# Weight tiles split over their whole width, and the products with a tile's low part issued last, in a diffusion layer on one Trainium2 core

## The chip, the cores and the metric

The kernel runs on one core of one Trainium2 chip. The metric is the device time of one execution in microseconds (us); the median of three runs counts. Engines are named as in the profile: PE is TensorE's matmul stream and PEld its weight loads, DVE is VectorE, ACT is ScalarE, POOL is GpSimd, SP is SyncE, which here only issues DMAs.

## What is computed

One layer of a diffusion backbone over 256 latent tokens and 256 context tokens, width 2048, all in float32: a half-step SwiGLU feed-forward block (FFN1, 5632 hidden channels), a token mixer (attention heads beside mLSTM heads), a second half-step feed-forward block (FFN2, latent tokens only), each behind an RMS norm whose shift, scale and gate come from a condition vector through `w_mod`.

```python
def half_step_ffn(x, mod, i, g, w_up, w_down):
    h = adaln(x, g, mod, i)
    a, b = jnp.split(h @ w_up, 2, axis=-1)
    return x + 0.5 * mod[:, i + 2, None, :] * ((jax.nn.silu(a) * b) @ w_down)
...
    mod_l = (silu_c @ w_mod[l] + b_mod[l]).reshape(B, N_MOD, D_MODEL)
    xl = half_step_ffn(xl, mod_l, 0, ...); xc = half_step_ffn(xc, mod_c, 0, ...)
    ...                                    # projections w_in, mLSTM, attention, w_out
    xl = half_step_ffn(xl, mod_l, 6, ...)
    return rms_norm(xl, g_final)
```

## The kernel before

**Products in three parts.** A float32 product is made of three matmuls on float32r operands (`mm3`, L138): each operand x is kept as hi (x rounded to float32r) and lo (x minus hi), and hi·hi, hi·lo and lo·hi are added up in one PSUM bank. Tokens are split once and kept; weights are split as they arrive. A weight tile is 128 x 2048, 1 MB, loaded by one DMA into one of three `raw` buffers (or accumulated by POOL's DMAs into one of two `chain` buffers, which hold sums of weight blocks).

**The split (L110).** `split` works on each half of the tile, 1024 wide: ACT copies the half to `hi` (L118), DVE subtracts (L119) to get `lo`. `hi` and `lo` have four buffers of 1024 each, so two tiles' worth. A buffer is free again when the last matmul that reads it is done.

**Two ways round.** With `hhi`/`hlo` (tokens) moving, the weights stand still; in the feed-forward blocks the tokens stand still and the weights move, 512 columns at a time. Per step of the contraction, `mm3` issues (token hi, weight hi), (token hi, weight lo), (token lo, weight hi).

**FFN1's quads.** Most of FFN1's first half (`quad`, called ten times, n = 1 to 10) makes four products of blocks out of seven (Strassen-Winograd form). A quad goes through seven entries `m`, each with two weight tiles `q`, so 14 tiles. For each tile the products of token block s = 0 are issued, then those of s = 1: 2 x 4 x 3 = 24 matmuls of 512 columns. The entries, their token forms, and the PSUM banks that they add to, two banks each (s = 0, 1):

```python
            order = (
                (a11, held, X, True, chained(1, 0), p1),
                (a12, plain, Z, True, None, c11),
                (n1, held, Y, True, chained(1, 2), kept),
                (s4, loaded, Y, False, lambda q: accum(ra[q], part(n, 1, q)), p35),
                (s2, held, X, False, chained(0, 2), c12),
                (s3, lambda q: ra[q], X, False, None, c22),
                (a22, held, Y, True, again, c21),
            )
```

The fourth value says whether the banks begin afresh. Two neighbours share banks: s4 adds to the Y that n1 has just filled, and s3 to the X that s2 has just filled. In between, the last function of the entry reads the bank: `kept(s)` is an ACT copy of Y to `cy` (L765); `c12(s)` is a DVE addition of X to `c12` (L744) and a multiplication (L745). So the first s4 matmul on Y[0] has to wait for `kept(0)`, and the first s3 matmul on X[0] for the addition of `c12(0)`. `c21(s)` at the quad's end is a DVE addition, an ACT Silu (L783) and a DVE multiplication; its result is transposed on PE by `turned()` (L739), called after the products of s = 0 in the first tile (q = 0) of an entry, so in the next quad's first tile for s = 0.

**Side work.** Beside the quads, DVE reduces tiles of `w_mod` (128 x 1024, `sraw`, two buffers, loaded by SP at L227): two `SCALAR_TENSOR_TENSOR` operations per tile (L198), one tile per step of a quad in most steps.

**What sets the order.** The kernel's framework lists each engine's instructions before the launch, by its own scheduler; on the chip each engine's list is fixed, with semaphore waits. At the start (before 150 us) PE and DVE are held to the order of the source.

**Other stages.** FFN1's second half (`pair`, five times) runs the same seven entries over two column blocks c, so that two neighbours on one bank have a whole tile of the other column block between them. The token projections (`project`, `channels`) follow, then the mixer, `out_proj`, and FFN2, where quads of one token block alternate with ordinary tiles (`units`).

Of the kernel before, what the change touches and what calls it, by code (L numbers as in the profile page):

```python
# [19 lines left out]
P = 128  # L20
# [29 lines left out]
def tile_layer(ctx: ExitStack, tc: tile.TileContext, I: dict, out: bass.AP):  # L50
# [59 lines left out]
    def split(raw, n=2048):  # L110

        half = n // 2
        parts = []
        for h in range(2):
            hi = wp.tile([P, 1024], F32R, tag="hi", name="hi", bufs=4)[:, :half]
            lo = wp.tile([P, 1024], F32R, tag="lo", name="lo", bufs=4)[:, :half]
            src = raw[:, h * half : (h + 1) * half]
            nc.scalar.activation(hi, src, AF.Copy)  # L118
            vector[0].tensor_tensor(lo, src, hi.bitcast(F32), op=ALU.subtract)  # L119
            parts.append((hi, lo))  # L120

        def at(w):
            h, o = divmod(w.start, half)
            return tuple(x[:, o : o + w.stop - w.start] for x in parts[h])

        return at
# [11 lines left out]
    def mm3(out_ap, sh, sl, mh, ml, first, last, skip=False):  # L138

        tensor[0].matmul(out_ap, sh, mh, start=first, stop=False, skip_group_check=skip)  # L140
        tensor[0].matmul(out_ap, sh, ml, start=False, stop=False, skip_group_check=skip)  # L141
        tensor[0].matmul(out_ap, sl, mh, start=False, stop=last, skip_group_check=skip)  # L142
# [257 lines left out]
    def products(wup, pre, k0, k1, hhi, hlo, early=False):  # L400

        n = (k1 - k0) * P
        most = min(2 * NPRE, 2048 // n // 2 * 2)

        def load(u0):
            nu = min(most, 2 * NPRE - u0)
            raw = raw_tile(n * nu)  # L410
            tc.keep_in_program_order(
                nc.sync.dma_start(
                    raw.rearrange("p (u c) -> p u c", u=nu),
                    wup[u0 // 2 : (u0 + nu) // 2, :, :, k0 * P : k1 * P].rearrange("f a p c -> p (f a) c"),
                )
            )
            return raw, nu

        ahead = load(0)
        if early:  # L420
            wt = split(ahead[0], n * ahead[1])
        yield
        for u0 in range(0, 2 * NPRE, most):
            raw, nu = ahead
            if u0 or not early:
                wt = split(raw, n * nu)
            if u0 + most < 2 * NPRE:
                ahead = load(u0 + most)
            for u in range(nu):
                b = pre[(u0 + u) // 2][u % 2]  # L430
                for k in range(k0, k1):
                    w = slice(u * n + (k - k0) * P, u * n + (k - k0 + 1) * P)
                    mm3(b, *wt(w), hhi[:, k, :], hlo[:, k, :], k == 0, k == KT - 1)
                yield
# [207 lines left out]
    with pool(name="f1u", bufs=1) as f1u:  # L642
# [26 lines left out]
        for f in range(NPRE, FB):  # L669
            pab = []  # L670
            for ab in range(2):
                wt = load_split(I["w_up1"][f, ab])
                b = bank()
                for k in range(KT):
                    mm3(b, *wt(slice(k * P, (k + 1) * P)), hhi[:, k, :], hlo[:, k, :], k == 0, k == KT - 1)
                pab.append(b)
            tail(f, pab)
# [72 lines left out]
        def quad(n, after=lambda step: None):  # L750
# [198 lines left out]
    def pair(p):  # L949
# [73 lines left out]
        for m, (g, src, dst, fresh, then, use) in enumerate(order):  # L1023
            a = place0[m] if p == 0 and m < 2 else place[g]
            for c in range(2):
# [8 lines left out]
                if p == NP - 1:  # L1034
# [5 lines left out]
                    if m in (1, 4, 6):  # L1040
                        gates = used[c] = ahead.pop(0)
                    elif m == 5:
                        gates = used[c]
                for s in range(2):
                    if fresh:
                        dst[c, s] = tbank() if c and dst is not X else bank()
                    for j in range(FB):
                        k = slice((FB * s + j) * P, (FB * s + j + 1) * P)
                        mm3(dst[c, s], a[:, 0, k], a[:, 1, k], *wt(slice(j * CB, (j + 1) * CB)), fresh and j == 0, j == FB - 1, True)
# [5 lines left out]
    def block_products(b, wt, t):  # L1055
        for j in range(FB):
            w = slice((FB * t + j) * P, (FB * t + j + 1) * P)
            mm3(b, hid10[0][:, w], hid10[1][:, w], *wt(slice(j * CB, (j + 1) * CB)), j == 0, j == FB - 1)
# [12 lines left out]
    def last1():  # L1071
# [3 lines left out]
        for s in (CTX, LAT):  # L1075
            for i, (_, cb) in [(i, x) for i, x in enumerate(LAST) if x[0] == s]:
# [7 lines left out]
                for t in range(2 * s, 2 * s + 2):  # L1084
                    b = bank()
                    block_products(b, wt, t)
# [18 lines left out]
    def products_of(bs, wt, n, ks, toks):  # L1105

        for j, k in enumerate(ks):
# [24 lines left out]
    with ExitStack() as mx:  # L1132
# [165 lines left out]
        def channels(name, h, N, b):  # L1298

            wt = load_split(I[name][h])  # L1300
            for k in range(KT):
                w = slice(k * P, (k + 1) * P)
                mm3(b, *wt(w), hhi[:, k, 512 - N :], hlo[:, k, 512 - N :], k == 0, k == KT - 1)
                if k % 4 == 3:
                    next(beside["part"], None)
                    yield
# [336 lines left out]
        def out_proj(cb, gs, bs):  # L1643
            bs.extend(bank() for _ in range(2))
            for n, g in enumerate(gs):
                wt = load_split(I["w_out"][cb, g])
                for j in range(4):
                    k = 4 * g + j
                    w = slice(j * CB, (j + 1) * CB)
                    for t in range(2):  # L1650
                        tt = slice(t * P, (t + 1) * P)
                        mm3(bs[t], chi2[:, k, tt], clo2[:, k, tt], *wt(w), n == 0 and j == 0, n == len(gs) - 1 and j == 3)
                    yield
# [109 lines left out]
    with f2x:  # L1763
# [28 lines left out]
        for f in range(NPRE, FB):  # L1792
            pab = []
            for ab in range(2):
                wt = load_split(I["w_up2"][f, ab])
                b = bank()[:, :T]
                for k in range(KT):
                    mm3(b, *wt(slice(k * P, (k + 1) * P)), h2hi[:, k, :T], h2lo[:, k, :T], k == 0, k == KT - 1)
# [110 lines left out]
        def quad(n):  # L1909
# [65 lines left out]
            for m, (a, src, dst, fresh, then, use) in enumerate(order):  # L1975
                for q in range(2):
# [3 lines left out]
                    if then:  # L1980
                        then(q)
                    for j in range(4):
                        k = 4 * q + j
                        mm3(B[dst], a[0][:, k, :], a[1][:, k, :], *wt(slice(j * CB, (j + 1) * CB)), fresh and k == 0, k == 7, True)
# [4 lines left out]
        def up(n):  # L1989

            sab = []
            for ab in range(2):
                bs = [bank() for _ in range(2)]
                for u in range(4):
                    wt = load_split(part(n, ab, u))
                    for j in range(4):
                        k = 4 * u + j
                        w = slice(j * CB, (j + 1) * CB)
                        for t in range(2):
                            tt = slice(t * P, (t + 1) * P)  # L2000
                            mm3(bs[t], h2hi[:, k, tt], h2lo[:, k, tt], *wt(w), k == 0, k == KT - 1)
# [10 lines left out]
        def block(n, wt, t):  # L2012

            b = bank()
            tt = slice(t * P, (t + 1) * P)
            for j in range(FB):
                w = slice(j * CB, (j + 1) * CB)
                mm3(b, hids[n][0][:, j, tt], hids[n][1][:, j, tt], *wt(w), j == 0, j == FB - 1)
            return b
# [3 lines left out]
        def down(n):  # L2023

            assert (n, 1) in done or not n
            for cb in range(NCB):
                wt = load_split(I["w_dn2"][n, cb])
                for t in range(2):
                    c = slice(cb * CB, (cb + 1) * CB)
                    b = block(n, wt, t)  # L2030
# [51 lines left out]
        def last2():  # L2082
# [13 lines left out]
            for t in range(2):  # L2096
                ss = sm.tile([P, 4], F32, tag="ss4", name="ss4", bufs=4)
                for cb in range(NCB):
                    c = slice(cb * CB, (cb + 1) * CB)
                    b = block(LAST, parts[cb], t)  # L2100
# [109 lines left out]
```

## Time and profile before

| | |
|---|---|
| three runs | 2667.7 us median (2666.27 to 2670.44) |
| span of the profiled execution | 2666.8 us, 0.9 us below the median; no other time is recorded for it |
| granted TensorE clock, mean | 0.996 |
| PE busy | 2609.9 us (98%), 12718 matmuls, each with a weight load of its own (PEld x12718) |
| DVE / ACT / POOL busy | 2130.1 us (80%) / 1347.2 us (51%) / 221.6 us (8%) |
| DMA | 679.97 MB, mean 255 GB/s |

A matmul's record lasts longer than the step to the next one, since matmuls overlap; the step is what counts. In a timeline, a row is start, duration, engine, line, operation, out<-in, and in brackets the idle time before it with what ended that.

### The profile page before, as it was taken

How to read it: one execution, taken by the hardware profiler on the slowest of the kernel's cores; microseconds unless marked ns; L12 is line 12 of the kernel's file. 1: busy time of each engine (PE TensorE's matmuls, PEld its weight loads, DVE VectorE, ACT ScalarE, POOL GpSimd, SP SyncE). 2: the span in 40 equal slices, each digit the busy share in tenths (PEclk: the TensorE clock that was granted, in tenths of full speed). 3: DMA queues.
4: the chain of work that ended last, by engine and by line, in shares of the span. 5: the costliest groups of instructions: out<-in, count | busy, mean ns of one | idle time of the engine just before them, and what ended most of it. 6: DMA issues, size and time to landing. Idle time of an engine off the chain costs nothing. (4 is left out here: it accounts for less than half of the span.)

```text
span 2666.8 us, 33730 instructions
## 1 busy us (share of the span) xinstructions
PE 2609.9 (98%) x12718; PEld 2158.4 (81%) x12718; DVE 2130.1 (80%) x2901; ACT 1347.2 (51%) x1682; POOL 221.6 (8%) x271
## 2 busy tenths in 40 slices
PE   8999999999999999999999999999999999999998
PEld 4688887888888878888889888877888888888886
DVE  5797878878888788888886979797688777777867
ACT  4354444544444565444454346355476655555554
POOL 0000001100000100000110000121000000000001
PEclk9999999999999999999999999999999999999999
DMA  9979999999999989889986866574579998989975
GB/s 346 351 213 270 263 279 260 258 276 281 264 280 273 266 230 239 229 209 234 225 233 224 309 229 225 205 260 166 172 249 284 295 286 292 289 277 281 277 230 168
DMA packets 135027, 679.97 MB, mean 255 GB/s; under 512 B 14152, under 2 KB 23624, under 8 KB 73552
## 3 DMA queue, kind: packets, MB, share of 16 engines
q1 hardware_dynamic: 107504, 500.59, 50.9%
q0 software_dynamic: 27360, 177.22, 34.0%
q8 instruction: 100, 1.64, 0.2%
q14 instruction: 63, 0.52, 0.1%
HBM read 659.87 MB, written 17.89 MB: 254 GB/s over the span
## 5 line engine op out<-in xcount | busy, mean ns | idle before, releaser
L118 ACT ACTIVATE hi<-raw 128x1024 fp32r<-128x1024 f32 (+3 forms) x542 | 560.7, 1038 | 639.0 <-PE mm L142 473.0
L119 DVE TENSOR_TENSOR lo<-raw,hi 128x1024 fp32r<-128x1024 f32 (+1 forms) x524 | 630.0, 1209 | 277.2 <-ACT hi L118 260.0
L118 ACT ACTIVATE hi<-chain 128x1024 fp32r<-128x1024 f32 x320 | 337.5, 1059 | 259.1 <-PE mm L142 129.1
L119 DVE TENSOR_TENSOR lo<-chain,hi 128x1024 fp32r<-128x1024 f32 x320 | 387.4, 1222 | 97.6 <-ACT hi L118 95.0
L140 PE MATMUL mm<-hi,hhi 128*128 128x512 f32 (+3 forms) x1024 | 392.5, 385 | 6.5 <-DVE c L744 6.0
L141 PE MATMUL mm<-lo,hhi 128*128 128x512 f32 (+3 forms) x1024 | 388.0, 379 | 1.7 <-DVE lo L119 1.5
L142 PE MATMUL mm<-hi,hlo 128*128 128x512 f32 (+3 forms) x1024 | 387.5, 379 | 0.0
L198 DVE SCALAR_TENSOR_TENSOR junk<-sraw,cBh 128x1024 fp8e5<-128x1024 f32 x192 | 234.4, 1221 | 23.2 <-DMA sraw<-in_w_mt 20.9
L140 PEld LDWEIGHTS mm<-hi,hhi 128*128 128x128 f32 x1024 | 192.8, 189 | 39.5 <-ACT hi L118 4.5
L141 PEld LDWEIGHTS mm<-lo,hhi 128*128 128x128 f32 x1024 | 193.1, 189 | 33.9 <-DVE lo L119 2.8
L142 PEld LDWEIGHTS mm<-hi,hlo 128*128 128x128 f32 x1024 | 192.8, 188 | 33.8
L142 PE MATMUL mm<-hi,hid2l 128*128 128x512 f32 x352 | 137.3, 390 | 0.0
L140 PE MATMUL mm<-hi,hid2h 128*128 128x512 f32 x352 | 137.2, 390 | 0.0
L141 PE MATMUL mm<-lo,hid2h 128*128 128x512 f32 x352 | 137.1, 390 | 0.0
L140 PE MATMUL mm<-hi,h2hi 128*128 128x512 f32 x320 | 125.0, 391 | 1.5 <-DVE sab L1802 1.5
L141 PE MATMUL mm<-lo,h2hi 128*128 128x512 f32 x320 | 124.6, 390 | 0.0
L142 PE MATMUL mm<-hi,h2lo 128*128 128x512 f32 x320 | 124.6, 389 | 0.0
L641 POOL DMA_DIRECT2D chain<-in_w_up1b x60 | 53.0, 883 | 742.3 <-DVE lo L119 606.9
L142 PE MATMUL mm<-hhi,lo 128*128 128x512 f32 (+1 forms) x288 | 100.4, 349 | 4.5 <-DVE lo L119 4.4
L140 PE MATMUL mm<-hhi,hi 128*128 128x512 f32 (+1 forms) x288 | 101.2, 351 | 0.0
L141 PE MATMUL mm<-hlo,hi 128*128 128x512 f32 (+1 forms) x288 | 99.5, 345 | 0.0
L198 DVE SCALAR_TENSOR_TENSOR sr<-sr,cBl 128x1024 f32<-128x1024 f32 x72 | 87.2, 1218 | 7.6 <-DMA sr<-in_w_mt 7.3
(474 smaller groups left out, 5499.3 us busy)
## 6 DMA issues: line engine op xcount, KB each, us to landing
raw<-in_w_dn SPq DMA_DIRECT2D x70, 1024.0 KB, 7.4
sraw<-in_w_mt SPq DMA_DIRECT2D x128, 512.0 KB, 7.5
chain<-in_w_up1b POOLq DMA_DIRECT2D x60, 1024.0 KB, 10.7
raw<-in_w_up2b SPq DMA_DIRECT2D x50, 1024.0 KB, 7.0
raw<-in_w_up1b SPq DMA_DIRECT2D x40, 1024.0 KB, 8.5
sr<-in_w_mt SPq DMA_DIRECT2D x69, 512.0 KB, 5.3
mraw<-in_w_m SPq DMA_DIRECT2D x32, 1024.0 KB, 7.2
chain<-in_w_dn POOLq DMA_DIRECT2D x30, 1024.0 KB, 8.7
```

Source lines behind the costliest of these rows:

```text
L118: nc.scalar.activation(hi, src, AF.Copy)
L119: vector[0].tensor_tensor(lo, src, hi.bitcast(F32), op=ALU.subtract)
L140: tensor[0].matmul(out_ap, sh, mh, start=first, stop=False, skip_group_check=skip)
L141: tensor[0].matmul(out_ap, sh, ml, start=False, stop=False, skip_group_check=skip)
L142: tensor[0].matmul(out_ap, sl, mh, start=False, stop=last, skip_group_check=skip)
L198: ins = nc.vector.scalar_tensor_tensor(junk() if junk else raw, raw, 1.0, cB[s], op0=ALU.mult, op1=ALU.mult, accum_out=mT[:, i, s, kt, h : ...
L641: accum = lambda dst, src: nc.gpsimd.dma_start(dst, src, accum_op=ALU.add)
```

## The change

`split` makes `hi` and `lo` of a tile by one ACT and one DVE instruction over its whole width; the buffers are two of 2048 instead of four of 1024. `mm3` gives way to a class `Products`, which collects a tile's matmuls in two lists: `early` holds the two that need the tile's high part, `late` the one that needs its low part. All callers issue a tile's early products first and its late ones last. Where one tile serves two banks (two token blocks), the order is early of both, then late of the first, its evacuation, late of the second, its evacuation. The number of matmuls, and what they add up, stays the same.

```diff
     def split(raw, n=2048):
 
-        half = n // 2
-        parts = []
-        for h in range(2):
-            hi = wp.tile([P, 1024], F32R, tag="hi", name="hi", bufs=4)[:, :half]
-            lo = wp.tile([P, 1024], F32R, tag="lo", name="lo", bufs=4)[:, :half]
-            src = raw[:, h * half : (h + 1) * half]
-            nc.scalar.activation(hi, src, AF.Copy)
-            vector[0].tensor_tensor(lo, src, hi.bitcast(F32), op=ALU.subtract)
-            parts.append((hi, lo))
...
+        hi = wp.tile([P, 2048], F32R, tag="hi", name="hi", bufs=2)[:, :n]
+        lo = wp.tile([P, 2048], F32R, tag="lo", name="lo", bufs=2)[:, :n]
+        nc.scalar.activation(hi, raw, AF.Copy)
+        vector[0].tensor_tensor(lo, raw, hi.bitcast(F32), op=ALU.subtract)
+        return lambda w: (hi[:, w], lo[:, w])
...
-    def mm3(out_ap, sh, sl, mh, ml, first, last, skip=False):
-
-        tensor[0].matmul(out_ap, sh, mh, start=first, stop=False, skip_group_check=skip)
-        tensor[0].matmul(out_ap, sh, ml, start=False, stop=False, skip_group_check=skip)
-        tensor[0].matmul(out_ap, sl, mh, start=False, stop=last, skip_group_check=skip)
+    class Products:
...
+            a, b = ((sl, mh), (sh, ml)) if self.moving else ((sh, ml), (sl, mh))
+            self.early += [go(sh, mh, first, False), go(*a, False, False)]
+            self.late.append(go(*b, False, last))
+
+        def run(self, late=None):
+            todo = self.late if late else self.early if late is not None else self.early + self.late
...
@@ quad @@
+                    ops = [Products(True), Products(True)]
                     for s in range(2):
                         for j in range(4):
                             k = 4 * q + j
                             hi, lo = a[0][:, s, k, :], a[1][:, s, k, :]
-                            mm3(dst[s], hi, lo, *wt(slice(j * CB, (j + 1) * CB)), fresh and k == 0, k == 7, True)
+                            ops[s].add(dst[s], hi, lo, *wt(slice(j * CB, (j + 1) * CB)), fresh and k == 0, k == 7, True)
+                        ops[s].run(False)
+                        if not s and not (q and use):
+                            turned()
+                    for s in range(2):
+                        ops[s].run(True)
                         if q and use:
                             use(s)
-                        elif not s:
-                            turned()
...
@@ products_of @@
+        ops = Products(True)
         for j, k in enumerate(ks):
             w = slice(j * n, (j + 1) * n)
             for t in toks:
                 tt = slice(t * P, (t + 1) * P)
-                mm3(bs[t], hhi[:, k, tt], hlo[:, k, tt], *wt(w), k == 0, k == KT - 1)
+                ops.add(bs[t], hhi[:, k, tt], hlo[:, k, tt], *wt(w), k == 0, k == KT - 1)
+        for _ in ops.in_parts(len(ks)):
             next(beside["part"], None)
             yield
```

`pair`, `products`, `channels`, `out_proj`, `up`, `block` and `last1` are changed in the same way.

The lists of instructions move at three places that matter below. First ACT, in a quad, where the entry n1 ends and s4 begins; `cy` is what `kept` writes, the `raw` tiles are those of s4. Before:

```order
L118 ACTIVATE hi_2880<-raw_2878 128x1024
L118 ACTIVATE hi_2884<-raw_2878 128x1024
L765 ACTIVATE cy_2862<-mm_2798 128x512
L118 ACTIVATE hi_2919<-raw_2917 128x1024
L765 ACTIVATE cy_2876<-mm_2799 128x512
L118 ACTIVATE hi_2923<-raw_2917 128x1024
```

And after:

```order
L114 ACTIVATE hi_2700<-raw_2698 128x2048
L114 ACTIVATE hi_2735<-raw_2733 128x2048
L780 ACTIVATE cy_2690<-mm_2626 128x512
L780 ACTIVATE cy_2696<-mm_2627 128x512
L114 ACTIVATE hi_2768<-chain0_1273 128x2048
```

Both copies of Y now stand behind the whole high part of s4's second tile; before, the first copy stood ahead of it. All ten quads have this order.

Second DVE, in the same quads, where s2 ends and s3 begins; `c12` is the addition that reads X, `raw_2878` (after: `raw_2698`) is s3's first tile. Before:

```order
L119 TENSOR_TENSOR lo_3035<-raw_2878,hi_3034 128x1024
L119 TENSOR_TENSOR lo_3039<-raw_2878,hi_3038 128x1024
L198 SCALAR_TENSOR_TENSOR junk8_1314,mT_94<-sraw_2967,cBh_1315 128x1024
L744 TENSOR_TENSOR c12_2940<-mm_2624,c12_2940 128x512
L198 SCALAR_TENSOR_TENSOR junk8_1314,mT_94<-sraw_2967,cBh_1315 128x1024
L745 TENSOR_TENSOR ca_2696<-ca_2696,c12_2940 128x512
```

And after:

```order
L115 TENSOR_TENSOR lo_2839<-raw_2698,hi_2838 128x2048
L210 SCALAR_TENSOR_TENSOR junk8_1278,mT_94<-sraw_2775,cBh_1279 128x1024 x2
L759 TENSOR_TENSOR c12_2760<-mm_2468,c12_2760 128x512
L759 TENSOR_TENSOR c12_2766<-mm_2469,c12_2766 128x512
L760 TENSOR_TENSOR ca_2540<-ca_2540,c12_2760 128x512
```

The addition for X[0] now stands behind both operations of the side work, not behind one. Eight of the ten quads have the two operations there; in the other two the addition follows the subtraction directly.

Third PE at that place, before (the last matmuls of s2 on X[1] and the first of s3 on X[0]; `s2h`, `s2l`, `hhi`, `hlo` are the token parts):

```order
L140 MATMUL mm_2625<-hi_2997,s2h_1454 128x512
L141 MATMUL mm_2625<-lo_2998,s2h_1454 128x512
L142 MATMUL mm_2625<-hi_2997,s2l_1455 128x512
L140 MATMUL mm_2624<-hi_3034,hhi_101 128x512
L141 MATMUL mm_2624<-lo_3035,hhi_101 128x512
```

And after:

```order
L137 MATMUL mm_2468<-lo_2802,s2h_1410 128x512 x4
L137 MATMUL mm_2469<-lo_2802,s2h_1410 128x512 x4
L137 MATMUL mm_2468<-hi_2838,hhi_101 128x512
L137 MATMUL mm_2468<-hi_2838,hlo_102 128x512
L137 MATMUL mm_2468<-hi_2838,hhi_101 128x512
```

X[0] (before mm_2624, after mm_2468) is now complete four matmuls ahead of s3, where it was twelve.

More of the change, by code (lines that the diff above doesn't have):

```diff
@@ L432, in products @@
                     w = slice(u * n + (k - k0) * P, u * n + (k - k0 + 1) * P)
-                    mm3(b, *wt(w), hhi[:, k, :], hlo[:, k, :], k == 0, k == KT - 1)
-                yield
+                    ops.add(b, *wt(w), hhi[:, k, :], hlo[:, k, :], k == 0, k == KT - 1)
+            yield from ops.in_parts(nu)
     xsrc = {CTX: I["ctx"], LAT: I["x"]}
@@ L1300, in channels @@
             wt = load_split(I[name][h])
+            ops = Products(False)
             for k in range(KT):
                 w = slice(k * P, (k + 1) * P)
[L1303 to L1306, printed above, removed]
+                ops.add(b, *wt(w), hhi[:, k, 512 - N :], hlo[:, k, 512 - N :], k == 0, k == KT - 1)
+            for _ in ops.in_parts(4):
+                next(beside["part"], None)
+                yield
         todo = []
@@ L1651, in out_proj @@
                         tt = slice(t * P, (t + 1) * P)
[L1652 to L1653 removed]
+                        ops.add(bs[t], chi2[:, k, tt], clo2[:, k, tt], *wt(w), n == 0 and j == 0, n == len(gs) - 1 and j == 3)
+                yield from ops.in_parts(4)
         def residual(cb, bs):
```

69 lines of the change are left out of this document (51 added, 18 removed).

## The prediction

> **What bounds the kernel now.** I read the page first, then the busy time by stage, then who PE waits for, then timelines of the quads.
>
> ```profile
> span 2666.8 us, 33730 instructions
> PE 2609.9 (98%) x12718; PEld 2158.4 (81%) x12718; DVE 2130.1 (80%) x2901; ACT 1347.2 (51%) x1682; POOL 221.6 (8%) x271
> ```
>
> ```profile
> 150.00:300.00 150.00, 149.97 (x669) 123.90 (x668) 126.23 (x143) 74.47 (x85) 14.22 (x16) 1.00 0.92 237
> 300.00:950.00 650.00, 644.04 (x2894) 531.33 (x2893) 533.64 (x681) 315.74 (x364) 56.37 (x64) 1.00 0.97 272
> 950.00:1400.00 450.00, 444.92 (x2007) 368.01 (x2006) 379.08 (x431) 229.09 (x267) 54.61 (x64) 1.00 0.88 226
> 1400.00:2000.00 600.00, 580.28 (x3235) 505.08 (x3234) 481.21 (x929) 295.49 (x446) 47.87 (x59) 0.99 0.65 227
> 2000.00:2640.00 640.00, 640.00 (x2862) 529.36 (x2862) 493.08 (x521) 361.10 (x376) 41.84 (x48) 1.00 0.90 276
> ```
>
> PE is the bound: it idles 2666.8 - 2609.9 = 57 us in all. Of those, 6 us lie in the quads (300 to 950), 5 in FFN1's second half, 20 in the projections and the mixer, none in FFN2; the rest is the start and the end. ACT and DVE have room, so fewer and longer splits buy nothing by themselves. The change issues the same matmuls, so it can only move PE's idle time. Who ends it:
>
> ```profile
> PE mm L140 <- DVE c L744: 6.0, 4, 2.1
> PE mm L142 <- DVE lo L119: 4.7, 4, 2.3
> PE mm L140 <- ACT hi L118: 4.0, 4, 2.7
> PE tr L141 <- DVE lo L119: 3.2, 2, 1.9
> PE mm L141 <- DVE lo L119: 2.1, 2, 1.5
> PE mm L78 <- DVE lo L78: 2.0, 7, 0.4
> ```
>
> (Engine and line that waits, what it waits for: us in total, times, longest.) Waits for a low part add up to 4.7 + 3.2 + 2.1 + 2.0 = 12.0 us, waits for a high part to 4.0, and `c12`'s addition holds PE back by 6.0 us in four of the ten quads.
>
> **What it may gain.** The low part is now needed only two thirds into a tile's matmuls (16 of 24 in a quad), so I let all 12.0 us go: **-12.0 us** (at least half, -6.0). In exchange the first matmul needs the whole high part.
>
> ```profile
> L119 DVE TENSOR_TENSOR lo<-raw,hi 128x1024 fp32r<-128x1024 f32 x500 | 609.1, 1224 | 266.1 <-ACT hi L118 248.9 <-PE mm L1294 12.2
> L118 ACT ACTIVATE hi<-raw 128x1024 fp32r<-128x1024 f32 x500 | 528.9, 1060 | 589.9 <-PE mm L142 440.5 <-PE mm L141 60.0 <-issue 25.4
> L118 ACT ACTIVATE hi<-raw 128x768 fp32r<-128x768 f32 x22 | 17.8, 839 | 33.3 <-PE mm L142 18.0 <-DMA raw<-in_w_up 11.1 <-DVE lo L119 4.2
> L78 DVE TENSOR_TENSOR lo<-raw,hi 128x768 fp32r<-128x768 f32 x14 | 12.7, 952 | 0.0
> ```
>
> From 768 to 1024 columns an ACT copy grows by 221 ns and a subtraction by 272 ns, so 2048 columns should take 1.06 + 4 x 0.221 = 1.94 us and 1.22 + 4 x 0.272 = 2.31 us. Each of the four waits for a high part grows by 1.94 - 1.06 = 0.88 us: **+3.5 us** (0 if the copy can start earlier). Two ops of 1224 ns against one of 2312 is 136 ns of fixed cost saved per tile, on an engine that is not the bound. [...]
>
> **Term A: n1 to s4, `kept`.** The change narrows the cover of an evacuation. In the fourth quad:
>
> ```profile
> 433.28 0.39 PE L142 MATMUL mm<-hi,n1l 128*128 128x512 f32 x1
> 433.51 0.39 PE L140 MATMUL mm<-hi,n1h 128*128 128x512 f32 x1
> 436.23 0.39 PE L140 MATMUL mm<-hi,s4h 128*128 128x512 f32 x1
> ```
>
> ```profile
> 433.71 0.60 ACT L765 ACTIVATE cy<-mm 128x512 f32<-128x512 f32 x1 [1.60 <-PE mm L142]
> 435.12 1.06 ACT L118 ACTIVATE hi<-raw 128x1024 fp32r<-128x1024 f32 x1 [0.81 <-PE mm L142]
> ```
>
> A matmul step is 433.51 - 433.28 = 0.227 us. Y[0] is complete with the matmul of 433.28; its copy starts 0.43 us after that issue, and s4 wants the bank 13 steps after it (436.23, 2.95 us). So now the copy is hidden. Afterwards only the four late matmuls of s = 1 stand between, so s4 wants Y[0] 5 steps = 1.13 us after Y[0]'s last issue; call that issue 0. On ACT the copy stands behind the high part of s4's second tile, whose buffer comes free with the last early matmul, 4 steps earlier: -0.91 + 0.43 = -0.48. It ends at 1.46. The copy overlaps it by some 0.1, takes 0.60 and ends near 1.96; PE goes on 0.14 later (that handover is seen in term B's rows) at 2.10. Wait: 2.10 - 1.13 = 0.97 us, in ten quads **+9.7 us** (0 if ACT were free at once: 0.43 + 0.60 + 0.14 = 1.17, the wait would be 0.04; up to 12 if the wide copy takes 0.2 us longer than I extend it to). That hangs on ACT keeping its list's order. In the rows, `cy` of 433.71 runs before the half of 435.12, as listed. [...]
>
> **Term B: s2 to s3, `c12`.** First a quad where the `w_mod` tile is in time, then one where it is late (DVE, then PE):
>
> ```profile
> 294.27 2.59 DVE L119 TENSOR_TENSOR lo<-raw,hi 128x1024 fp32r<-128x1024 f32 x2
> 296.77 1.22 DVE L198 SCALAR_TENSOR_TENSOR junk<-sraw,cBh 128x1024 fp8e5<-128x1024 f32 x1
> 297.92 0.69 DVE L744 TENSOR_TENSOR c<-mm,c 128x512 f32<-128x512 f32 x1
> ...
> 296.83 0.39 PE L142 MATMUL mm<-hi,s2l 128*128 128x512 f32 x1
> ```
>
> ```profile
> 458.31 1.23 DVE L198 SCALAR_TENSOR_TENSOR junk<-sraw,cBh 128x1024 fp8e5<-128x1024 f32 x1 [1.41 <-DMA sraw<-in_w_mt]
> 459.46 0.69 DVE L744 TENSOR_TENSOR c<-mm,c 128x512 f32<-128x512 f32 x1
> ...
> 457.76 0.39 PE L142 MATMUL mm<-hi,s2l 128*128 128x512 f32 x1
> 460.29 0.76 PE L140 MATMUL mm<-hi,hhi 128*128 128x512 f32 x1 [2.14 <-DVE c L744]
> ```
>
> Take X[0]'s last issue as 0 again (296.83 in the first). In time: afterwards the low part of s3's first tile gets its buffer with the last matmul of the tile before, 20 steps earlier, at -4.54 + 0.43 = -4.11, and DVE is through with it at -1.88 (ops overlap by 0.08). The two `SCALAR_TENSOR_TENSOR` take 2.46 us together, so the addition runs from 0.58 to 1.27 and PE goes on at 1.41: 0.28 us late. Late: there X[0]'s last issue was 12 steps before 457.76, at 455.04, and the side work began at +3.27. With both operations ahead the addition begins at 5.73, PE goes on at 6.56, 5.4 us after it wanted to; it was 2.3. So each late quad costs 3.1 us more: 1.3 for the second operation, 1.8 for the cover. With four late quads and four in time (two of the ten have no side work there) that is 4 x 3.1 + 4 x 0.28 = +13.5; if no transfer is late, 8 x 0.28 - 6.0 = -3.8. The transfers wait for the same DVE operations as before, and DMA is busy 0.97 of the time there (second number from the end in the row 300:950), so most should stay late; waits A stretch the loop a little. I take **+9.0 us**, three quarters of the way.
>
> **Term C: the quad's end, `c21`, and the transposes.**
>
> ```profile
> 639.16 0.69 DVE L744 TENSOR_TENSOR ca<-mm,ca 128x512 f32<-128x512 f32 x1
> 640.82 0.61 ACT L783 ACTIVATE ca<-ca 128x512 f32<-128x512 f32 x1
> 642.09 0.69 DVE L745 TENSOR_TENSOR ca<-ca,cy 128x512 f32<-128x512 f32 x1
> 643.69 0.60 PE L739 MATMUL tr<-ident,ca 128*128 128x128 f32 x4
> ```
>
> From Y[0]'s last issue to these transposes PE has 25 steps now, 13 + 12 = 5.7 us; afterwards 5 + 8 = 13 steps, 2.95 us. The bare chain is 0.43 + 0.69 + 0.61 + 0.69 and two handovers of about 0.1, 2.6 us, so it fits if both engines are free. DVE has the low part of the next quad's first tile and a pair of side work in front. From 0 to 1.8 us per quad in nine quads, 0 to 16; I take 0.5, since the pair begins early there when buffers come in time: **+4.5 us**.
>
> **The rest.** FFN1's second half and FFN2 have a tile of other work (at least 24 steps, 5.4 us) between two uses of a bank, so the 1.8 us of lost cover is hidden by that tile; without it each would cost about what A does. At the end of a projection all four banks are complete within four matmuls, which may hold up the next one; 0 to 4 us, I take 0, nearest to the full cover that two free banks of six give.
>
> Sum on the profiled execution: 2666.8 - 12.0 + 3.5 + 9.7 + 9.0 + 4.5 = 2681.5; the median of the runs lies 0.9 above that execution's span: **2682 us**, +0.5%.
>
> **The rivals.**
> *The late low part wins (faster).* If the `w_mod` tiles arrive in time once PE pauses at A, B turns to -3.8, C is 0, and high parts come no later: 2667.7 - 12.0 + 9.7 - 3.8 = 2661.6, and less if A is partly hidden. It decides when B's transfers land before X[0] is complete. For it: DVE sheds 136 ns a tile, and the waits for low parts are real. Against it: DMA share 0.97 in the quads.
> *DVE falls behind at the quad's end (slower still).* With C at 1.8 us in nine quads, B at its 13.5 and projections at 4: 2667.7 - 12.0 + 3.5 + 9.7 + 13.5 + 16 + 4 = 2702. For it: DVE is busy 82% of the quads' time and the chain's window is halved.
> *Nothing changes.* A is hidden because ACT gets its buffer earlier than I think, gains and losses cancel: 2668. Against it: the starts in term A follow the buffers' release by 0.43 us.
>
> **How the numbers follow.** The forecast has 0.48, the faster rival 0.17, the slower one 0.22, no change 0.08, and 0.05 stays for more than all my upper bounds. The low end is the faster rival rounded down a little, 2660, the high end 2708: all upper bounds together, 2667.7 - 6 + 3.5 + 12 + 13.5 + 16 = 2707, rounded up; beyond them some 0.15 is left. Within 0.2%, which is 5.3 us and about what measurements of this kernel can tell from no change, lies the third rival. Faster 0.17, same 0.08, slower 0.48 + 0.22 + 0.05 = 0.75.
>
> **What would show it.** A right: a wait of PE for the ACT copy to `cy` of about 1 us in ten quads; wrong: none. B right: the wait for `c12`'s addition grows from 6.0 us towards 20. C right: waits of PE's transposes for `ca` appear. Gain right: waits for low parts vanish, those for high parts grow below 4 us. The prediction is wrong if PE's idle time in the quads does not grow, or if FFN2, where PE is never idle now, shows idle time.

## The result: slower by 1.1%, twice the forecast, and the profile after

The changed kernel takes 2697.2 us (median of four runs, 2691.1 to 2700.4) against 2667.9 us of the kernel before beside it: ratio 1.0108, 95% interval 1.0092 to 1.0124, 29.3 us more. The forecast was 14.3 us more. The profiled execution has a span of 2694.3 us, 27.5 us more than that of before. The head of its page:

```profile
span 2694.3 us, 32490 instructions
PE 2617.3 (97%) x12718; PEld 2160.1 (80%) x12718; DVE 2098.3 (78%) x2450; ACT 1265.7 (47%) x1233; POOL 223.8 (8%) x271
```

The busy time by stage, the windows shifted so that they hold the same matmuls as those of before (columns: window; length; busy time and count of PE, PEld, DVE, ACT, POOL; granted clock; DMA share; GB/s):

```profile
155.00:308.50 153.50, 150.82 (x669) 123.33 (x667) 124.23 (x118) 71.21 (x59) 14.26 (x16) 1.00 0.90 238
308.50:977.00 668.50, 651.52 (x2894) 533.06 (x2895) 525.06 (x566) 293.02 (x250) 56.51 (x64) 0.99 0.95 264
977.00:1422.50 445.50, 443.83 (x2007) 368.42 (x2006) 374.02 (x350) 214.94 (x189) 53.25 (x64) 1.00 0.90 230
1422.50:2025.00 602.50, 579.57 (x3234) 504.04 (x3233) 477.01 (x862) 286.00 (x378) 51.07 (x58) 0.99 0.64 223
2025.00:2666.00 641.00, 640.89 (x2862) 529.03 (x2861) 480.61 (x368) 331.16 (x224) 41.13 (x47) 1.00 0.89 276
```

The 2894 matmuls that took 650.0 us before take 668.5 us now, and PE idles 17.0 us among them instead of 6. FFN1's second half (third row) is shorter by 4.5 us, the projections and the mixer longer by 2.5, FFN2 is as it was (the table below cuts the stages at other places). Who PE waits for, largest first (us in total, times, longest):

```profile
PE mm L137 <- DVE c L759: 11.1, 4, 3.5
PE mm L137 <- ACT cy L780: 6.7, 10, 0.7
PE tr L1569 <- DVE pr L1563: 5.5, 3, 2.1
PE tr L78 <- DMA mraw<-in_w_m: 5.5, 4, 1.6
PE mm L137 <- DVE lo L115: 3.9, 2, 2.6
PE mm L78 <- DVE hlo L78: 3.8, 4, 1.7
PE mm L137 <- ACT hi L114: 3.2, 6, 1.3
...
PE tr L754 <- DVE ca L760: 1.3, 2, 1.1
```

A is the second row, B the first, C the last one: all three are there. Waits for low parts fell from 12.0 to 3.9 us, but rows that the prediction had not named grew: the mixer's `pr` (attention's weights, made on ACT and DVE and transposed on PE; 2.5 us before) and the transfers of `w_m` at the start (`mraw`, 0.6 us before).

Where the time went is best read by counting matmuls, since both kernels issue 12718 in the same sequence of stages. The table gives, for each part, how much longer it took than in the kernel before, worked out from the start of the same-numbered matmul at its two ends in the two traces. The columns end with matmul 990, counted from 0 (149.8 us before: the start, taken from the first matmul), 4600 (960.7: quads), 6420 (1377.8: `pair` and the last column block), 7250 (1522.2: norm and first projections), 9390 (1943.1: the rest of the projections, mixer, `out_proj`) and the last one (2655.2: FFN2). For the changed kernel they add up to 26.1 of the 27.5 us; the rest lies outside the first and the last matmul. The kernels below the first are the experiments.

| kernel | start | quads | pair, last block | norm, projections | mixer | FFN2 | median us |
|---|---|---|---|---|---|---|---|
| changed | +5.0 | +22.3 | -5.0 | +4.3 | +0.3 | -0.8 | 2697.2 |
| split_only | +4.3 | +6.0 | +10.3 | +0.6 | +20.5 | +111.4 | 2819.0 |
| order_only | +2.3 | +7.8 | -5.0 | +7.2 | -6.1 | +1.5 | 2678.1 |
| quad_old | +3.5 | +5.8 | -4.5 | +3.3 | +2.0 | +1.9 | 2676.6 |
| hi_halves | +0.1 | +13.1 | -5.0 | +1.4 | +3.2 | +0.9 | 2684.8 |
| skip10 | +2.4 | +8.1 | -4.6 | +1.6 | +3.3 | 0.0 | 2682.1 |
| fixed | +3.5 | -0.8 | -4.3 | +2.2 | +0.4 | -0.6 | 2670.7 |
| mix_halves | +0.7 | +23.5 | -4.9 | +3.1 | -0.2 | +3.6 | 2694.1 |
| before_skip10 | 0.0 | -6.2 | +1.5 | -1.5 | +1.3 | -0.4 | 2662.6 |
| pair_new | -0.3 | -4.0 | -5.0 | +0.2 | +2.1 | -1.4 | 2659.5 |
| order_skip10 | -0.7 | -1.0 | -3.3 | +6.8 | -5.9 | +0.9 | 2668.0 |
| last1_old | -2.9 | +2.0 | -3.0 | +1.8 | -6.0 | +0.1 | 2667.3 |
| mix_new | +2.0 | +1.6 | -1.0 | +2.2 | -6.4 | +0.4 | 2666.1 |
| start_new | -1.5 | +1.6 | -0.1 | -1.5 | -0.5 | +0.5 | 2669.0 |
| best | +0.5 | -6.1 | -1.9 | +1.5 | -6.6 | +0.4 | 2655.9 |

Each row is one execution. Kernels with the same start differ by up to 5 us there (changed, quad_old, hi_halves, skip10, fixed, mix_halves: +0.1 to +5.0), and parts that are alike differ by up to 4 us in the other columns, so only larger differences, or such as several rows repeat, are read from it. The kernel before ran at 2668.1 to 2668.8 us beside the experiments.

### The profile page after: what moved, and what is told of

It is laid out like the page before. It is cut to its first block, busy times and chain, and to the rows that moved or that the text cites. A ratio compares the mean times of both kernels' runs of the same rounds, so it can differ in the third digit from the quotient of the medians.

```text
span 2694.3 us, 32490 instructions
## 1 busy us (share of the span) xinstructions
PE 2617.3 (97%) x12718; PEld 2160.1 (80%) x12718; DVE 2098.3 (78%) x2450; ACT 1265.7 (47%) x1233; POOL 223.8 (8%) x271
## 4 chain that ended last, share of the span: by engine, by line
PE 75%; DVE 7%; DMA 4%; ACT 2%; issue 2%; POOL 1%; ACTq 0%; POOLq 0%; DVEq 0%; SPq 0%
PE mm L137 60%; PE Y L137 4%; PE tr L137 4%; PE X L137 3%; DVE lo L115 2%; DMA sraw<-in_w_mt 2%; ACT hi L114 1%; DVE sr L210 1%; DMA sr<-in_w_mt 1%; PE tr L754 1%; DVE junk L210 1%; DVE cy L1306 0%; PE mm L1578 0%; POOL rstd L160 0%; PE tr L1923 0%
## 5 line engine op out<-in xcount | busy, mean ns | idle before, releaser
L114 ACT ACTIVATE hi<-raw 128x2048 fp32r<-128x2048 f32 (+4 forms) x271 | 507.9, 1874 | 664.8 <-PE mm L137 500.5
L115 DVE TENSOR_TENSOR lo<-raw,hi 128x2048 fp32r<-128x2048 f32 (+3 forms) x262 | 593.2, 2264 | 205.2 <-ACT hi L114 164.5
L114 ACT ACTIVATE hi<-chain 128x2048 fp32r<-128x2048 f32 x160 | 307.1, 1919 | 379.1 <-PE mm L137 225.4
L115 DVE TENSOR_TENSOR lo<-chain,hi 128x2048 fp32r<-128x2048 f32 x160 | 366.2, 2289 | 93.6 <-ACT hi L114 92.8
L137 PE MATMUL mm<-lo,hhi 128*128 128x512 f32 (+3 forms) x1024 | 243.5, 381 | 3.9 <-DVE lo L115 3.9
L978 DVE TENSOR_TENSOR acc<-acc,mm 128x512 f32<-128x512 f32 x108 | 71.4, 685 | 34.8 <-PE mm L137 34.8
L137 PE MATMUL mm<-hi,sumshl 128*128 128x512 f32 x400 | 94.7, 389 | 0.0
L137 PE MATMUL mm<-hlo,hi 128*128 128x512 f32 (+1 forms) x288 | 93.7, 343 | 0.0
L137 PE MATMUL mm<-lo,hid2h 128*128 128x512 f32 x352 | 88.2, 390 | 0.0
```

The lines of the kernel that those rows point to most:

```text
L114: nc.scalar.activation(hi, raw, AF.Copy)
L115: vector[0].tensor_tensor(lo, raw, hi.bitcast(F32), op=ALU.subtract)
L137: return lambda: tensor[0].matmul(out_ap, st, mv, start=start, stop=stop, skip_group_check=skip)
L978: nc.vector.tensor_tensor(col(t, cb), col(t, cb), b, op=ALU.add)
```

## The experiments

**The change in its two parts.** split_only is the kernel before with this alone:

```diff
-        half = n // 2
-        parts = []
...
+        hi = wp.tile([P, 2048], F32R, tag="hi", name="hi", bufs=2)[:, :n]
+        lo = wp.tile([P, 2048], F32R, tag="lo", name="lo", bufs=2)[:, :n]
```

> The kernel before with the whole-width split alone (two buffers of 2048 each); the products keep their old order, 12 matmuls of one token block, then 12 of the other, hi and lo mixed. Theory 1 (the loss in the quads comes from the order of the products, which shortens the time between a bank's last matmul and the next use of it): no wait for the copies to cy (Y[0] is complete 13 steps = 2.95 us before s4), the wait for c12's addition stays near the 6.5 us of before, the quads stay within 5 us of before, and the whole lies at 2668 to 2676 us. Theory 2 (the wide split by itself makes PE wait, because a tile's second matmul now needs the whole low part, which can begin only after the high part of 1.9 us and takes 2.3 us): waits for lo appear in the quads, the whole lies above 2685 us.

order_only is the changed kernel with that edit reversed:

> The changed kernel with the old split in two halves (four buffers of 1024); only the order of the products is new. Theory 1: the quads lose as much as in the changed kernel, 18 to 22 us, since both halves of s4's second tile stand ahead of the copies to cy as the whole did (2 x 1.06 us against 1.9): waits for cy of about 1 us in ten quads, c12 waits near 13 us; the whole at 2685 to 2697 us. Theory 2: the halves bring the time back, the whole at 2660 to 2670 us.

quad_old is the changed kernel with `mm3` and the old loop in `quad`:

> The changed kernel with the old order of products in the ten quads alone. Theory 1: the 22 us that the quads lost come back, the whole at 2673 to 2677 us, and the 5 us lost outside the quads stay. Theory 2: the quads lose again, by waits for lo, and the whole stays above 2685 us.

split_only took 2819.0 us (ratio 1.0565, interval 1.0547 to 1.0582), order_only 2678.1 (1.0030, 1.0015 to 1.0045), quad_old 2676.6 (1.0036, 1.0023 to 1.0050). In the quads theory 1 comes nearer: +6.0, 1 us above its bound, with no wait for `cy`, and quad_old brings back 16.5 of the 22.3 us. But the waits for low parts that theory 2 named are there too, 6.5 us in split_only and 4.5 in quad_old, seven in each. For the whole, theory 2 names the mechanism, and its largest part sits where neither theory looked. PE's waits in split_only, in all and from 2020 us on (FFN2):

```profile
PE mm L131 <- DVE lo L115: 95.4, 79, 3.9
...
```

```profile
PE mm L131 <- DVE lo L115: 74.6, 64, 1.6
```

L131 is the second of the three matmuls of a product. It needs the low part, which now comes after a high part of 1.92 us and takes 2.29 itself (means of the same operations in the changed kernel, 1917 and 2295 ns). In FFN2's quads a tile has 12 matmuls, 2.7 us at 0.227 a step, and FFN2 has 64 such waits. With the low part's products last these begin 8 steps, 1.8 us, into such a tile; the longest wait of 1.6 us, which begins one step in, ends about there, and the waits are gone in the changed kernel. So the two parts of the change are not two gains: the wide split alone costs 151 us, and the new order gives back 122 of it, at a price of its own.

order_only came out between the two theories, and its quads lose 7.8 us where theory 1 said 18 to 22: there is no row of waits for `cy`. Half a tile's buffer is free four matmuls earlier, so ACT begins s4's second tile 0.9 us sooner (in the fourth quad at 437.80, 1.34 us ahead of Y[0]'s last issue, against 0.48 in the changed kernel), and the copy is in time: it runs from 439.71 to 440.29, and s4 begins at 440.34, 0.06 us after it could have begun. Term A needs the new order and the wide split together.

**Term A alone.** hi_halves changes one thing in the changed kernel: the copies to `hi` of s4's two tiles are made in two halves.

```diff
-        nc.scalar.activation(hi, raw, AF.Copy)
+        for h in range(2) if two else ():
+            half = slice(h * (n // 2), (h + 1) * (n // 2))
+            nc.scalar.activation(hi[:, half], raw[:, half], AF.Copy)
+        if not two:
+            nc.scalar.activation(hi, raw, AF.Copy)
...
-                    wt = split(src(q))
+                    wt = split(src(q), two=m == 3)
```

> The changed kernel; only the high parts of s4's two tiles are copied in two halves on ACT, so that in the list the first copy to cy stands behind one half of 1.06 us and ahead of the other. If term A is the wide copy ahead of the evacuation: the first half runs from -0.48 to 0.58, the copy from there to 1.18, PE goes on at 1.3 and wanted to at 1.13: the wait falls from 0.97 to 0.2 us a quad, 8 us less in all, about 2689 us. If it is the shortened cover alone, whatever stands on ACT: 0.97 us a quad stay, 2697 us.

The fourth quad, ACT and then PE, first in the changed kernel (start, duration):

```profile
448.99 1.92 ACT L114 ACTIVATE hi<-raw 128x2048 fp32r<-128x2048 f32 x1 [3.47 <-PE mm L137]
450.81 1.06 ACT L780 ACTIVATE cy<-mm 128x512 f32<-128x512 f32 x2
...
448.79 1.98 PE L137 MATMUL mm<-lo,n1h 128*128 128x512 f32 x8
451.44 0.50 PE L137 MATMUL mm<-hi,s4h 128*128 128x512 f32 x1 [0.67 <-ACT cy L780]
451.78 0.40 PE L137 MATMUL mm<-hi,s4l 128*128 128x512 f32 x1
```

Then in hi_halves:

```profile
437.67 1.06 ACT L116 ACTIVATE hi<-raw 128x1024 fp32r<-128x1024 f32 x1 [3.38 <-PE mm L141]
438.63 0.58 ACT L784 ACTIVATE cy<-mm 128x512 f32<-128x512 f32 x1
439.11 1.05 ACT L116 ACTIVATE hi<-raw 128x1024 fp32r<-128x1024 f32 x1
...
437.47 1.97 PE L141 MATMUL mm<-lo,n1h 128*128 128x512 f32 x8
439.28 0.48 PE L141 MATMUL mm<-hi,s4h 128*128 128x512 f32 x1
```

In the changed kernel s4 could have begun 8 steps after 448.79, at 450.61; it began at 451.44, and its first step is 0.34 us instead of 0.227: 0.94 us. In hi_halves it could have begun at 439.29 and did. The quads went from +22.3 to +13.1 us, 9.2 us for ten quads; the whole to 2684.8 us (1.0064, 1.0045 to 1.0082). What held PE was the wide copy ahead of the evacuation, not the shortened cover by itself.

**Term B alone.** skip10 leaves the `w_mod` step out of s3's first tile (step 10 of 14, in the first and the last quad too) and spreads it over the other steps; before_skip10 is the same edit on the kernel before, order_skip10 on order_only.

```diff
-        side = mod_items(half_items(2, 5), nc.sync.dma_start, sraw, 2, cond, lambda: junk8, ((96, (NB - 2) * 14 - 2),), 0)
+        side = mod_items(half_items(2, 5), nc.sync.dma_start, sraw, 2, cond, lambda: junk8, ((96, (NB - 2) * 13 - 2),), 0)
...
-            quad(n, lambda step: steps(side))
+            quad(n, lambda step: step != 10 and steps(side))
```

> The changed kernel; no w_mod tile is reduced in the first step of s3, and the others are spread over the remaining 13 steps of a quad, so that nothing stands between s3's low part and the addition of c12 on DVE. If term B is the two reductions, late by their transfers, ahead of the addition: the 13 us of waits for c12 (3.7, 2.3, 3.1, 2.6 and four of 0.35) fall below 3, the whole at 2684 to 2688 us. Rival: the late transfers only hold DVE up at another step, and PE waits for a low part or another bank there instead: above 2692 us.

> The same edit on the kernel before: its four waits for c12 (1.8, 2.3, 1.4, 1.0 = 6.5 us) should go, 2661 to 2663 us. Rival as above: 2667 to 2669 us.

> The changed kernel with half-width splits and the edit on w_mod: the new order of products everywhere, with neither A nor B. The order alone took 2678 us, of that 8.7 us of waits for c12: 2669 to 2671 us if they go. If the new order had a gain that only B hid, it would fall below 2663 us.

The third quad of the changed kernel, DVE and then PE:

```profile
388.24 1.23 DVE L210 SCALAR_TENSOR_TENSOR junk<-sraw,cBh 128x1024 fp8e5<-128x1024 f32 x1 [3.24 <-DMA sraw<-in_w_mt]
...
389.51 1.22 DVE L210 SCALAR_TENSOR_TENSOR junk<-sraw,cBh 128x1024 fp8e5<-128x1024 f32 x1
...
390.66 1.28 DVE L759 TENSOR_TENSOR c<-mm,c 128x512 f32<-128x512 f32 x2
...
386.01 1.97 PE L137 MATMUL mm<-lo,s2h 128*128 128x512 f32 x8
391.50 0.77 PE L137 MATMUL mm<-hi,hhi 128*128 128x512 f32 x1 [3.52 <-DVE c L759]
```

DVE waits 3.24 us for the transfer, then does both reductions, and only then adds X to `c12`. In skip10 a single row of that wait is left in the quads:

```profile
PE mm L137 <- ACT cy L780: 6.7, 10, 0.7
PE tr L754 <- DVE ca L760: 4.0, 4, 1.7
PE mm L137 <- DVE c L759: 0.4, 1, 0.4
```

skip10 took 2682.1 us (1.0047, 1.0031 to 1.0062), the quads 14.2 us less than in the changed kernel; before_skip10 2662.6 us (0.9969, 0.9959 to 0.9980), so 6 us of this were in the kernel before as well; order_skip10 2668.0 us (0.9993, 0.9983 to 1.0003). skip10 lies 2 us below the range expected, order_skip10 1 us below its own. The late transfers did not come back as a wait of that size elsewhere, only C grew from 1.3 to 4.0 us.

fixed has both repairs:

> The changed kernel with both repairs, s4's high parts copied in halves and no w_mod tile in s3's first step. If A and B are all that the quads lost, the quads return to within 3 us of the kernel before; 21 us less than the changed kernel and some 4 us more at the start and in the mixer than before: 2669 to 2675 us. If they are not additive (the one wait covers the other): above 2678 us.

2670.7 us (1.0006, 0.9994 to 1.0017), the quads at -0.8: the two repairs add up, 23.1 us together where each alone took 9.2 and 14.2. But they are not all that the new order costs in the quads, since the edit on `w_mod` also takes away 6 us that the kernel before had. With that edit the quads stand at -4.0 to -6.2 where their order is old (before_skip10, pair_new, best) and at -1.0 to +2.0 where it is new and neither A nor B is left (fixed, order_skip10, last1_old). Some 5 us remain. In fixed PE waits in the quads only here:

```profile
PE tr L758 <- DVE ca L764: 2.7, 3, 1.1
PE mm L141 <- DVE c L763: 1.3, 1, 1.3
```

The transposes of term C (0.4 us of waits in before_skip10) are a part of it; the rest stays open.

**Where the 12 us of waits for low parts went.** start_new and mix_new are the kernel before, half-width splits, with the new order in one place alone: in `products`, or in `products_of`, `channels` and `out_proj`.

> The kernel before with the new order of products at the start alone (products, before 150 us). As the prediction has it: the seven waits for lo, 2.0 us, vanish and the start is 2 us shorter, 2666 us. Theory (PE then runs into the transfers of w_m, mraw): those waits rise from 0.6 us to 3 to 5 us, the start is 0 to 4 us longer, 2668 to 2672 us.

> The kernel before (half-width splits) with the new order of products in the projections and the mixer alone. Waits for lo there are 4.4 + 1.5 = 5.9 us in the kernel before. As the prediction has it (a wait that goes is time gained): they vanish, 2662 us. Theory (behind them stand the mixer's own chains on DVE and ACT, pr, hm, hcd, h, which end as late): lo waits fall below 1.5 us, the others grow by as much, 2667 to 2671 us.

The start (0 to 150 us) in start_new, where no row for `lo` is left:

```profile
PE tr L78 <- DMA mraw<-in_w_m: 4.0, 4, 1.4
...
```

Before, the row for `mraw` was this:

```profile
PE tr L78 <- DMA mraw<-in_w_m: 0.6, 2, 0.3
```

PE ran into the transfers of `w_m`: 2.0 us of waits for `lo` became 3.4 more for `mraw`. The ten executions with the new order at the start wait 3.0 to 5.5 us for `mraw`; of the six with the old one five wait 0 to 1.3, and mix_new 5.0, so that the transfers scatter by themselves too. The whole took 2669.0 us (1.0003, 0.9993 to 1.0014), so no gain is measured; the start itself was 1.5 us shorter in this execution, which lies within its scatter.

mix_new lies between the two theories. The projections and the mixer (1378 to 1945 us), before and then in mix_new:

```profile
PE mm L142 <- DVE lo L119: 4.4, 3, 2.3
PE tr L1539 <- DVE pr L1533: 2.5, 3, 1.1
...
PE mm L141 <- DVE lo L119: 1.5, 1, 1.5
...
PE tr L1389 <- DVE hm L1398: 0.8, 1, 0.8
```

```profile
PE tr L1420 <- DVE hm L1429: 3.2, 3, 1.4
PE tr L1570 <- DVE pr L1564: 3.1, 2, 2.2
...
PE mm L153 <- DVE lo L119: 0.8, 1, 0.8
```

Waits for `lo` fell from 5.9 to 0.8 us, those for `hm` (the output of the mLSTM heads) and `pr` grew by 2.4 and 0.6, and the two columns came out 4.2 us shorter together; the whole 2666.1 us (0.9988, 0.9979 to 0.9998), 2.5 us less. So a good part of the gain is there. In the changed kernel something takes it away, and two runs ask what.

**What takes the mixer's gain away.** last1_old is order_skip10 with the old order in the last column block of FFN1. mix_halves is the changed kernel, where from that block on and up to FFN2 both operations of a split are done in halves, in the same two wide buffers.

```diff
+        k = 2 if halves_on[0] else 1
+        for h in range(k):
+            c = slice(h * n // k, (h + 1) * n // k)
+            nc.scalar.activation(hi[:, c], raw[:, c], AF.Copy)
+            vector[0].tensor_tensor(lo[:, c], raw[:, c], hi[:, c].bitcast(F32), op=ALU.subtract)
```

> order_skip10 (the new order everywhere, half-width splits, edit on w_mod) with the old order in the last column block alone. If that block's new order, by which all its banks are complete late, holds up the norm and the projections behind it: the block loses 1.6 us and the projections and the mixer gain 5 us, 2664 to 2666 us against 2668. If not: 2668 to 2670 us.

> The changed kernel; behind the last column block and up to FFN2 the splits are done in two halves on ACT and DVE, in the same two wide buffers. If the mixer's own operations (pr and others) come late because a wide low part of 2.3 us stands ahead of them on DVE: the waits for pr fall from 5.5 to 3 us, projections and mixer lose 1 us and not 4.6, 2693 us. If it is the coarser release of the buffers: 2697 us.

Norm and first projections (1370 to 1520 us), order_skip10 and then last1_old (`acc` is the residual stream that the norm reads, `hcd` a small tile of the mLSTM gates):

```profile
PE tr L1281 <- DVE hcd L1276: 3.0, 1, 3.0
PE tr L392 <- ACT acc L183: 1.7, 1, 1.7
PE tr L392 <- DVE acc L185: 0.8, 1, 0.8
...
```

```profile
PE tr L1283 <- DVE hcd L1278: 1.5, 1, 1.5
...
PE tr L398 <- ACT acc L189: 0.2, 1, 0.2
```

The column for the norm goes from +6.8 to +1.8, the 5 us expected, and order_only, with the block new, has +7.2. An explanation, not shown by itself, is that with both banks of a tile complete only at its end the sums that the norm needs (`acc`, 1.7 + 0.8 us) are late. Two things speak against reading more from it: the medians, 2668.0 and 2667.3 us with spreads of 8 and 14 us, don't show it, and pair_new, which has this block new and the projections behind it old, waits 1.9 us for `acc` and stands at +0.2, only 1.7 above before_skip10. In the changed kernel that column is +4.3, and from +1.4 to +3.3 in its five relatives.

mix_halves took 2694.1 us (1.0095, 1.0080 to 1.0109). Its row for `pr`:

```profile
PE tr L1575 <- DVE pr L1569: 5.5, 2, 3.3
```

It has not fallen (5.5 us in the changed kernel too), so by this row and by the mixer's column the length of the operations is not the cause; the total is nearer to the 2693 us of that theory than to the 2697 of the other, but within the spread of the changed kernel, 2691.1 to 2700.4. The mixer's column sorts the kernels by their buffers: with the new order in the mixer and four of 1024 it is -5.9 to -6.6 (order_only, order_skip10, last1_old, mix_new, best), with two of 2048 -0.2 to +3.3 (the changed kernel, quad_old, hi_halves, skip10, fixed and mix_halves). What is left to take the gain away is the coarser release of the buffers; this is by elimination, since no run changes the number of buffers and nothing else.

**A faster kernel.** pair_new adds the new order in `pair` and the last column block to before_skip10. best has before_skip10's edit and the new order in `pair` and the mixer, without the last column block; both have half-width splits.

> The kernel before with that edit and with the new order of products, on half-width splits, in FFN1's second half alone (pair and the last column block), where all kernels with the new order gained 2.2 + 1.6 us and no bank is read between two neighbours. Theory 1 (early products first pays where a whole tile covers each evacuation): 3.8 us below the kernel before with the edit alone, 2657 to 2659 us, faster than both kernels. Rival (the time is taken back by what follows, as in the projections): equal to it, 2661 to 2663 us.

> The kernel before, half-width splits, no w_mod tile in s3's first step, and the new order of products in pair and in the projections and the mixer, not in the last column block. If the parts add up: -6 (the edit on w_mod) - 2.2 (pair) - 4.2 (mixer) = 2656 us, faster than every kernel so far. If the mixer takes the gain back as in pair_new: 2660 to 2663 us.

pair_new took 2659.5 us (0.9961, 0.9948 to 0.9975), not to be told from before_skip10 by its time; its column is -5.0. best took 2655.9 us (0.9949, 0.9937 to 0.9962), as the sum said, 12 us faster than the kernel before:

```profile
span 2654.1 us, 33796 instructions
```

## Why the prediction had the sign right and the size wrong

**Term A, +9.7: right, in its place, its mechanism and its size.** Ten waits; the copy to `hi` began 0.48 us ahead of Y[0]'s last issue (448.79 + 3 x 0.227 = 449.47), as forecast; 0.94 us each by the rows, 9.2 us taken away by hi_halves.

**Term B, +9.0: the mechanism right, the sum right by luck.** The late waits of before grew from 1.8, 2.3, 1.4 and 1.0 us to 3.7, 2.3, 3.1 and 2.6 (gaps between matmuls less a step), 5.1 together where 3.1 each was said; quads in time show four of 0.35 where 0.28 was said. The rest is the clock after these waits (last section), 3.4 us, for which the prediction had no term: 5.1 + 1.4 + 3.4 = 9.9. By the repairs the change's own share is 14.2 - 6.2 = 8.0.

**Term C, +4.5: mis-sized.** The transposes wait 1.3 us for `ca`; with B out of the way it is 4.0 in skip10 and 2.7 in fixed.

The quads: 23.2 forecast, 22.3 measured, so near only because the clock and the open rest make up for what the waits of B and C fell short. All the missing size lies outside them, where the two terms that were left, -12.0 and +3.5, make -8.5, and the trace shows 27.5 - 22.3 = +5.2.

**The gain, -12.0: this step failed.** It let every wait for a low part go for its full length, without naming what is late next. Of the 12.0 us, 8.1 went as waits. FFN1's second half kept what it gained (-5.0). At the start PE runs into the transfers of `w_m` (5.5 us of waits for `mraw`, 0.6 before). In the projections and the mixer the order by itself brings 4.2 of 5.9, and in the changed kernel these columns are 4.6 us longer instead.

**The wide split, +3.5: this step failed too.** It was priced at the four waits for a high part, as a duration, and these did not grow: 4.0 us before, 3.2 in six now. Its price in the mixer is some 6 us (+0.3 against -6.1 in order_only), put down by elimination to buffers that come free a whole tile at a time. With the old order the wide split costs 151 us, most of it in waits for the low part; the sum has no term for what the new order saves there. The start is longer too, by 0.1 to 5.0 us in six executions; that part stays open. The duration itself was close:

```profile
L115 DVE TENSOR_TENSOR lo<-raw,hi 128x2048 fp32r<-128x2048 f32 x250 | 573.7, 2295 | 191.6 <-ACT hi L114 162.7 <-issue 19.3 <-PE mm L137 4.7
L114 ACT ACTIVATE hi<-raw 128x2048 fp32r<-128x2048 f32 x250 | 479.3, 1917 | 605.8 <-PE mm L137 456.7 <-issue 41.0 <-DVE junk L210 24.4
```

2295 and 1917 ns, where 2312 and 1940 were said.

**"The rest", 0 for the end of a stage: doubtful at one place.** FFN2 stays hidden, as said (640.89 of 641.00 us busy). But the last column block hands over to the norm, and with half-width splits and the order new on both sides the norm's column is 5 us longer (order_skip10 against last1_old); with it new in the block alone it is not (pair_new).

The rival *the late low part wins* falls: the transfers stay late, and B does not turn. *Nothing changes* falls with the ten waits of A. *DVE falls behind at the quad's end* reaches nearly the measured time by another way: its C was 16 us and is 1.3.

## What to carry to other kernels

When a wait is to be removed, follow the waiting instruction to its second-latest operand before the gain is written down; here waits came back under another name, as one for a transfer (in start_new 2.0 us for `lo` became 3.4 more for `mraw`) or for a stage's own chain (in mix_new 5.1 us less for `lo`, 3.0 more for `hm` and `pr`). The wider operation cost more than its added duration at the waits that were there already (3.5 us by the forecast): 9.2 us went with the copy ahead of the evacuation, and with the old order the wide split cost 151. So ask which evacuation stands behind it in the engine's list, which product needs its whole result, and where its buffer is waited for. Two edits that are made together should be priced apart: here the new order undid most of the damage of the wide split, and what there was to gain, some 6 of the 12 us of best, lay in the new order without the wide split, in `pair` and in the mixer; the other 6 came from moving the side work.

## What was not expected of the hardware

A pause cost more than its length here. After the wait of term B that ends at 391.50 (3.52 us) the granted clock is 0.50, after the wait of term A in the fourth quad (0.67 us, to 451.44) it is 1.00 (windows of the changed kernel, with the granted clock third from the end):

```profile
391.50:393.50 2.00, 2.00 (x5) 1.61 (x6) 2.00 (x4) 0.00 (x0) 0.00 (x0) 0.50 1.02 426
451.00:452.00 1.00, 0.56 (x2) 0.48 (x3) 1.00 (x1) 0.88 (x2) 0.00 (x0) 1.00 0.94 233
```

In the first window the steps between matmuls are 0.43 us instead of 0.227. The clock's own record in the trace has it at 0.50 in the quads from 390.47 to 397.30, from 475.81 to 479.22 and from 718.15 to 721.57 us: for 6.83, 3.41 and 3.42 us. In the quads 23 such steps cost 4.6 us (6 and 1.2 before); rows of three or more of them cost 8.8 us in the whole trace (1.8 before): 7 of the 27.5 us lost are not waits at all. In the quads pauses of 2.3, 3.1 and 3.7 us were followed by it and one of 2.6 was not, nor were the ten of 0.83 us that A makes. What decides whether a pause is followed by it, no run shows.
